# State-space scan: the exponentials of the decays read from the banks of the spread decays, in place of a second spreading product

## The chip, the cores and the metric

The kernel runs on one core of a Trainium2 chip. Its time is the device time of one execution in microseconds (us); lower is better. The engines of a core run side by side, each with its own queue in order: TensorE (PE; its weight loads are shown as PEld), VectorE (DVE), ScalarE (ACT), GpSimd (POOL) and SyncE (SP), which issues most DMA transfers. Matrix products are written into PSUM banks (here 128 partitions x 512 floats), from which DVE and ACT read.

## The reference, cut to what matters

One inference step of a decoder layer: an input projection, a Mamba-2 state-space scan beside an mLSTM, cross attention and a gated feed-forward block, for a prompt of 512 tokens and 8 samples of 8 tokens. The change lies in the prompt's state-space scan. Per chunk, with `cum` the running sum of the log decays:

```
cum = cumsum(lac)                         # per head, over the tokens t of a chunk
lmat = exp(cum[t] - cum[s])  for s <= t   # decay from token s to token t
y_intra = (C_t . B_s * lmat * dt_s) x_s
y_inter = (C_t . h) * exp(cum[t])         # h: the state at the chunk's start
y = y_intra + y_inter
```

There are 16 heads of 64 channels, so two heads fill the 128 partitions.

## The kernel before, in words

The kernel uses chunks of 128 tokens, four for the prompt. The head pairs are worked in two groups of four (`ssd_prompt(0)` and `ssd_prompt(1)`, L654). A group first transposes its inputs (`ps_bt`, `ps_xt`), forms the scores (`ps_cb`) and carries the states through the chunks (`ps_h`, L680; `hs`, L686/L687). Then comes the loop over its head pairs (L690):

- For each head k of the pair, a spreading product `ps_l` (L697, bf16, 80 rows) puts `cum` of this head, for all 512 tokens, on all 128 partitions of one bank. `cumst` holds `cum` split into three bf16 parts, `sel` picks the head.
- DVE makes `lm` from it in four pieces (L700), ACT takes the exponential (L702), DVE multiplies by the scores (L703).
- `ps_yi` (L710): y_intra, for both heads, each with 64 output columns of the array side by side.
- `ps_ec` (L715): a second spreading product, once more `cum`, for tokens 128 to 511, head 0 on partitions 0 to 63 and head 1 on partitions 64 to 127; ACT takes its exponential `ec` (L718).
- `ps_yn` (L721): C . h for chunks 1 to 3; DVE multiplies `ec` by it (L723), DVE adds `ps_yi` to the skip term (L724), POOL adds `ec` (L725).

`ec` has a single buffer, `lm` has two. All the banks named here come from one pool of three (`MP`, L139).

The order of the work is not written out by hand in this part: a scheduler arranges each engine's instructions from the program, with priorities in program order and its own estimates of durations. So TensorE's rows mix the scan with the products of the input projection (L215, L216 and L218: high part, low part of the activations, low part of the weights) and of the values (`ps_v`, L882), whose weights ACT casts (L191) and whose low parts DVE or POOL make (L198, L196). The samples' scan (`ps_hs` L813 with 32 output columns, `ps_hu` L824) and, behind the last head pair, the mLSTM (`ps_d` L960, `ps_n` L983/L985, `ps_c` L988; for the samples `ps_ss` L1024, `ps_nh` L1042/L1049 with 32 output columns, `ps_cu` L1056) are mixed in as well. In the mLSTM, ACT and DVE both read the bank `ps_d` (L962, L966).

Of the kernel before, what the change touches and what calls it, by code (L numbers as in the profile page):

```python
# [11 lines left out]
F32 = mybir.dt.float32  # L12
F32R = mybir.dt.float32r
BF16 = mybir.dt.bfloat16
AF = mybir.ActivationFunctionType
# [4 lines left out]
P = 128  # L20
T = 576
TP = 512
# [93 lines left out]
def build(nc, tc, ctx, I, O):  # L116
    V, A, G, S, TE = nc.vector, nc.scalar, nc.gpsimd, nc.sync, nc.tensor
    mm = TE.matmul
# [20 lines left out]
    def MP(name="m"):  # L139
        return pa.tile([P, 512], F32, name=name, tag="a")  # L140

    def BP(name="b"):
        return pb.tile([P, 512], F32, name=name, tag="b")
# [15 lines left out]
    def C16(k):  # L159
        a, b = _c16[k]  # L160
        return c16[:, a:b]

    def PAR(k, j=None, w=1):
        a, b = _cols[k]
        return par[:, a:b] if j is None else par[:, a + j:a + j + w]
# [42 lines left out]
    def gemm(ps, units, xh, xl, t0, n, k0=0, k1=None, order=None, late=0):  # L208


        tiles = [(hi[:, j * P:(j + 1) * P], lo[:, j * P:(j + 1) * P]) for hi, lo, nk in units for j in range(nk)]
        order = order or range(len(tiles))
        for i, k in list(enumerate(order))[k0:k1]:
            (wh, wl), ah, al = tiles[k], xh(k, t0, n), xl(k, t0, n)
            mm(ps, wh, ah, start=i == 0, stop=False)  # L215
            products.append(mm(ps, wh, al, start=False, stop=False))  # L216
            for c in range(late) if i == late - 1 else [i] if i >= late else ():
                m = mm(ps, tiles[order[c]][1], xh(order[c], t0, n), start=False, stop=c == len(tiles) - 1)  # L218
        return m
# [97 lines left out]
    sel = C16("sel")  # L317
# [74 lines left out]
    stop = gemm(ps0[2][1], [(*w2, KT)], U, UL, 256, 320, 0, NSS)  # L392
# [13 lines left out]
    stop = gemm(ps0[3][1], [(*w3, KT)], U, UL, 256, 320, 0, 2)  # L406
# [40 lines left out]
    cumst = bcp.tile([80, T], BF16, name="cumst")  # L447
# [166 lines left out]
    with tc.issue_after(products[140].ins), tc.high_priority(offset=1000):  # L614
# [9 lines left out]
        pse = MP("ps_en")  # L624
# [6 lines left out]
        pse = MP("ps_en2")  # L631
# [17 lines left out]
    sd = st.enter_context(tc.tile_pool(name="ssd", bufs=1, reuse_waits="tile"))  # L649
# [4 lines left out]
    def ssd_prompt(g):  # L654
        Bt, Ct = bc[:, g, :], bc[:, 2 + g, :]
        ps = MP("ps_bt")
        for c in range(4):
            TE.transpose(ps[:, c * P:(c + 1) * P], Bt[:, c * P:(c + 1) * P], ident)
        btok = sd.tile([P, 4, P], F32, name="btok", tag="btok")
        A.copy(btok, ps.rearrange("p (c k) -> p c k", c=4))  # L660
        ps = MP("ps_cb")
        for c in range(4):
            m = mm(ps[:, c * P:(c + 1) * P], Bt[:, c * P:(c + 1) * P], Ct[:, c * P:(c + 1) * P], start=True, stop=True,
                   skip_group_check=True)
        outer.append(m)
        cbs = sd.tile([P, 512], F32, name="cbs", tag="cbs")
        A.copy(cbs, ps)
        xdt, hs = [], [None]
        for c in range(4):
            ps = MP("ps_xt")  # L670
            for j in range(4):
                TE.transpose(ps[:, j * P:(j + 1) * P], xs[:, g * 4 + j, c * P:(c + 1) * P], ident)
            xd = sd.tile([P, 8, 64], F32, name="xdt", tag="xdt", bufs=4)
            V.tensor_tensor(xd, ps.rearrange("p (h k) -> p h k", h=8),
                            CT[:, c, 32 + 8 * g:40 + 8 * g].unsqueeze(2).to_broadcast([P, 8, 64]), op=ALU.mult)
            xdt.append(xd)
            xe = sd.tile([P, 8, 64], F32, name="xe", tag="xe", bufs=1)
            G.tensor_tensor(xe, xd, wend[:, c, 8 * g:8 * g + 8].unsqueeze(2).to_broadcast([P, 8, 64]), op=ALU.mult)
            ps = MP("ps_h")
            states.append(mm(ps, btok[:, c, :], xe.rearrange("p h k -> p (h k)"), start=True, stop=True))  # L680
            h = sd.tile([P, 8, 64], F32, name="hs", tag="hs", bufs=4)
            p3 = ps.rearrange("p (h k) -> p h k", h=8)
            if c == 0:
                V.tensor_copy(h, p3)
            else:
                G.tensor_tensor(h, hs[c], decp[:, c, 8 * g:8 * g + 8].unsqueeze(2).to_broadcast([P, 8, 64]), op=ALU.mult)  # L686
                V.tensor_tensor(h, h, p3, op=ALU.add)  # L687
            hs.append(h)
        S.dma_start(O["ssmp"][:, g * 512:(g + 1) * 512], hs[4].rearrange("p h k -> p (h k)"))
        for j in range(4):  # L690
            jj = g * 4 + j
            psi = MP("ps_yi")
            lms = []
            for k in range(2):
                h = 2 * jj + k
                psb = MP("ps_l")
                mm(psb, sel[:80, h:h + 1].to_broadcast([80, P]), cumst[:, 0:TP], start=True, stop=True)  # L697
                lm = sd.tile([P, 512], F32, name="lm", tag="tmp", bufs=2)
                for c in range(4):
                    V.scalar_tensor_tensor(lm[:, c * P:(c + 1) * P], psb[:, c * P:(c + 1) * P], ncum[:, c, h:h + 1],  # L700
                                           C16("maskp"), op0=ALU.add, op1=ALU.add)
                exps.append(A.activation(lm, lm, AF.Exp))  # L702
                mults.append(V.tensor_tensor(lm, lm, cbs, op=ALU.mult))  # L703
                lms.append(lm)
                if len(mults) == 8:
                    G.tensor_copy(sd.tile([P, 1], F32, name="lm0"), lm[:, 0:1])

            for c in range(4):
                for k in (1, 0):
                    m = mm(psi[64 * k:64 * k + 64, c * P:(c + 1) * P], xdt[c][:, 2 * j + k, :], lms[k][:, c * P:(c + 1) * P],  # L710
                       start=True, stop=True, skip_group_check=True)
            inner.append(m)
            pse = MP("ps_ec")
            for k in range(2):
                mm(pse[64 * k:64 * k + 64, 0:384], sel[:80, 2 * jj + k:2 * jj + k + 1].to_broadcast([80, 64]),  # L715
                   cumst[:, P:TP], start=True, stop=True, skip_group_check=True)
            ec = sd.tile([P, 384], F32, name="ec", tag="ec", bufs=1)
            A.activation(ec, pse[:, 0:384], AF.Exp)  # L718
            psn = MP("ps_yn")
            for c in range(1, 4):  # L720
                mm(psn[:, (c - 1) * P:c * P], hs[c][:, 2 * j:2 * j + 2, :].rearrange("p h k -> p (h k)"),  # L721
                   Ct[:, c * P:(c + 1) * P], start=True, stop=True, skip_group_check=True)
            V.tensor_tensor(ec, ec, psn[:, 0:384], op=ALU.mult)  # L723
            V.scalar_tensor_tensor(y[:, jj, 0:TP], xs[:, jj, 0:TP], PAR("dskip", jj), psi, op0=ALU.mult, op1=ALU.add)  # L724
            G.tensor_tensor(y[:, jj, P:TP], y[:, jj, P:TP], ec, op=ALU.add)  # L725

    inner, outer, exps, mults = [], [], [], []
    ssd_prompt(0)
    ssd_prompt(1)


# [15 lines left out]
    sd = st2.enter_context(tc.tile_pool(name="ssds", bufs=1, side="right", reuse_waits="tile"))  # L747
# [28 lines left out]
    for g in range(2):  # L776
        psb = BP("ps_ls")
        pb3 = psb.rearrange("p (h t) -> p h t", h=8)
        for h in range(8):
            mm(psb[:, h * TS:(h + 1) * TS], sel[:80, 8 * g + h:8 * g + h + 1].to_broadcast([80, P]), cumst[:, TP:T],  # L780
               start=h == 0, stop=h == 7, skip_group_check=True)
# [8 lines left out]
        for h in range(8):  # L790
            k, j = h % 2, (8 * g + h) // 2
            mm(psi[64 * k:64 * k + 64, j * TS:(j + 1) * TS], xdts[:, 8 * g + h, :], lm[:, h, :], start=True, stop=True,
               skip_group_check=True)
# [12 lines left out]
    for b in range(4):  # L806
# [3 lines left out]
        for g in range(2):  # L810
            for hb in (1, 0):
# [3 lines left out]
                   start=b == 0, stop=b == 3, skip_group_check=True)  # L815
# [141 lines left out]
    for h in range(4):  # L957
        q, k = qk[:, h, :], qk[:, 4 + h, :]
        psb = MP("ps_d")
# [10 lines left out]
        for c in range(4):  # L970
            mm(pss[:, c * P:(c + 1) * P], k[:, c * P:(c + 1) * P], q[:, c * P:(c + 1) * P], start=True, stop=True,
               skip_group_check=True)
# [37 lines left out]
    psb = BP("ps_ds")  # L1010
    pb3 = psb[:, 0:256].rearrange("p (h t) -> p h t", h=4)
    for h in range(4):
        mm(psb[:, h * TS:(h + 1) * TS], sel[:68, h:h + 1].to_broadcast([68, P]), sxst[:, TP:T], start=h == 0, stop=h == 3,
           skip_group_check=True)
# [22 lines left out]
    for hb in range(2):  # L1037
# [6 lines left out]
        for b in range(4):  # L1044
# [3 lines left out]
            for h in range(4):  # L1048
                mm(psn[32 * h:32 * h + 32, 0:257], qpad[:, h, bb, :], c0[:, h, 0:257], start=False, stop=b == 3,  # L1049
                   skip_group_check=True)  # L1050
# [1426 lines left out]
```

## Time and profile before

| | |
|---|---|
| median of 3 runs | 1074.99 us (1074.83 to 1075.98) |
| the profiled execution | 1074.69 us, of which 1072.9 us are its span |
| TensorE's granted clock, mean | 0.999 |
| the eight head pairs (first `ps_l` to the last add) | about 129 to 251 us of the span |

Rows of the chain give start (us), duration (us), engine, tile and line, and "xN" for N TensorE instructions; a float32 product counts as two of them. Rows of the timeline give start, duration, engine, line, operation, out<-in and, in brackets, how long the engine had been idle before and which instruction's end released it. Rows of a tile give the shortest, median and longest duration in ns.

### The profile page before, as it was taken

What the parts mean: (1) busy time and instruction counts of PE and PEld (TensorE: products, weight loads), DVE (VectorE), ACT (ScalarE), POOL (GpSimd) and SP (SyncE); (2) the same over time, 40 slices, a digit from 0 to 9 for tenths busy, and PEclk for the clock granted to TensorE, in tenths of its full rate; (3) what the DMA queues carried; (4) which work ended last, traced back from release to release, by engine and by line L of the source; (5) the groups of instructions that cost most, each with busy time, mean ns of one, the idle gap of its engine ahead of it and who ended that gap; (6) DMA issues with size and microseconds to landing.
All of it is one profiled execution on the core that took longest, in us unless ns stands there. A gap on an engine that the chain in (4) does not pass through costs nothing.

```text
span 1072.9 us, 20686 instructions
## 1 busy us (share of the span) xinstructions
PE 1063.1 (99%) x8096; PEld 1011.0 (94%) x8096; DVE 757.7 (71%) x1523; ACT 608.9 (57%) x1102; POOL 231.0 (22%) x305
## 2 busy tenths in 40 slices
PE   9999999999999999999999999999999999999997
PEld 8999887778999999999999989999999999999997
DVE  6798775658878774758755556766467887787556
ACT  7778523345654555655555445645566566656654
POOL 0454543313213111000154201100011111111000
PEclk9999999999999999999999999999999999999999
DMA  6776544425655349642468775743476687578532
GB/s 209 176 162 132 158 134 172 147 89 168 196 150 152 106 143 330 235 170 98 158 213 288 265 256 176 254 124 98 133 179 137 160 188 178 114 191 188 144 119 89
DMA packets 58965, 181.74 MB, mean 169 GB/s; under 512 B 6604, under 2 KB 12108, under 8 KB 58356
## 3 DMA queue, kind: packets, MB, share of 16 engines
q1 hardware_dynamic: 42884, 138.22, 38.7%
q0 software_dynamic: 15408, 41.43, 19.7%
q8 instruction: 63, 1.03, 0.4%
q10 hardware_dynamic: 576, 0.79, 0.2%
q14 instruction: 34, 0.28, 0.1%
HBM read 159.75 MB, written 20.65 MB: 168 GB/s over the span
## 4 chain that ended last, share of the span: by engine, by line
PE 98%; DVE 0%; DMA 0%; POOL 0%; issue 0%; ACT 0%; SPq 0%; DVEq 0%
PE ps_in L215 7%; PE ps_in L218 7%; PE ps_in L216 7%; PE ps_v L882 5%; PE ps_g L1946 3%; PE ps_u L1946 3%; PE ps_g L1945 3%; PE ps_o L218 3%; PE ps_o L216 3%; PE ps_u L1947 3%; PE ps_g L1947 3%; PE ps_o L215 3%; PE ps_u L1945 3%; PE ps_dn L1945 2%; PE ps_dn L1947 2%; PE ps_dn L1946 2%
## 5 line engine op out<-in xcount | busy, mean ns | idle before, releaser
L215 PE MATMUL ps_in<-uh,whi 128*128 128x320 f32 (+1 forms) x544 | 162.6, 299 | 0.0
L218 PE MATMUL ps_in<-uh,wlo 128*128 128x320 f32 (+1 forms) x544 | 161.6, 298 | 0.0
L216 PE MATMUL ps_in<-ul,whi 128*128 128x320 f32 (+1 forms) x544 | 161.1, 296 | 0.0
L191 ACT CAST whi<-raw 128x1024 fp32r<-128x1024 f32 (+1 forms) x104 | 105.4, 1015 | 93.3 <-PE ps_in L216 21.5
L198 DVE TENSOR_TENSOR wlo<-raw,whi 128x1024 fp32r<-128x1024 f32 (+2 forms) x97 | 95.3, 983 | 63.7 <-ACT whi L191 63.0
L215 PEld LDWEIGHTS ps_in<-uh,whi 128*128 128x128 f32 x544 | 102.3, 188 | 1.9 <-issue 0.8
L218 PEld LDWEIGHTS ps_in<-uh,wlo 128*128 128x128 f32 x544 | 102.2, 188 | 1.9 <-issue 1.3
L216 PEld LDWEIGHTS ps_in<-ul,whi 128*128 128x128 f32 x544 | 102.4, 188 | 0.5
L196 POOL DMA_DIRECT2D wlo<-win x31 | 27.2, 877 | 80.2 <-ACT wlo L195 69.9
L1945 PE MATMUL ps_g<-b,whi 128*128 128x288 f32 x144 | 42.4, 295 | 0.0
L1946 PE MATMUL ps_g<-b,whi 128*128 128x288 f32 x144 | 42.3, 294 | 0.0
L1946 PE MATMUL ps_u<-b,whi 128*128 128x288 f32 x144 | 42.2, 294 | 0.0
L1945 PE MATMUL ps_u<-b,whi 128*128 128x288 f32 x144 | 42.2, 294 | 0.0
L1905 DVE TENSOR_TENSOR wlo<-sw,whi 128x1024 fp32r<-128x1024 f32 (+1 forms) x26 | 29.6, 1139 | 16.8 <-ACT whi L1904 16.8
L1918 ACT CAST whi<-rawx 128x1024 fp32r<-128x1024 f32 (+1 forms) x26 | 25.6, 986 | 26.2 <-PE ps_dn L1946 13.3
L1895 ACT CAST whi<-raw 128x1024 fp32r<-128x1024 f32 (+1 forms) x26 | 25.6, 985 | 22.8 <-PE ps_g L1946 11.8
L215 PE MATMUL ps_xo<-qh,whi 128*128 128x288 f32 x128 | 38.2, 301 | 0.0
L216 PE MATMUL ps_xo<-ql,whi 128*128 128x288 f32 x128 | 37.8, 297 | 0.0
L218 PE MATMUL ps_o<-mixm_h,wlo 128*128 128x256 f32 (+1 forms) x128 | 37.5, 293 | 0.0
L216 PE MATMUL ps_o<-mixm_l,whi 128*128 128x256 f32 (+1 forms) x128 | 37.5, 293 | 0.0
L218 PE MATMUL ps_xq<-u2h,wlo 128*128 128x320 f32 (+1 forms) x128 | 37.5, 294 | 0.0
L218 PE MATMUL ps_o<-mixs_h,wlo 128*128 128x320 f32 (+1 forms) x128 | 37.4, 293 | 0.0
(788 smaller groups left out, 3855.6 us busy)
## 6 DMA issues: line engine op xcount, KB each, us to landing
raw<-win SPq DMA_DIRECT2D x35, 512.0 KB, 4.4
raw<-wout SPq DMA_DIRECT2D x17, 512.0 KB, 4.2
raw<-wxq SPq DMA_DIRECT2D x13, 512.0 KB, 4.7
raw<-wgate SPq DMA_DIRECT2D x13, 512.0 KB, 3.3
raw<-wup SPq DMA_DIRECT2D x13, 512.0 KB, 4.7
wlo<-win POOLq DMA_DIRECT2D x24, 256.0 KB, 5.6
kva<-vc SPq DMA_DIRECT2D x11, 512.0 KB, 5.9
raw<-wv SPq DMA_DIRECT2D x10, 512.0 KB, 4.0
```

The source lines that it names most:

```text
L191: casts.append(A.copy(hi[:, :n], raw[:, :n]))
L196: accs.append(G.dma_start(lo[:, a:b], src[:, a:b], accum_op=ALU.add))
L198: e.tensor_tensor(lo[:, a:b], raw[:, a:b], hi[:, a:b].bitcast(F32), op=ALU.subtract)
L215: mm(ps, wh, ah, start=i == 0, stop=False)
L216: products.append(mm(ps, wh, al, start=False, stop=False))
L218: m = mm(ps, tiles[order[c]][1], xh(order[c], t0, n), start=False, stop=c == len(tiles) - 1)
L882: mm(ps, a, b, skip_group_check=True, **kw)
L1895: s.c1 = A.copy(s.h1[:, s.all], s.r1[:, s.all])
L1905: V.tensor_tensor(s.l2[:, s.all], sw[:, s.all], s.h2[:, s.all].bitcast(F32), op=ALU.subtract)
L1945: mm(ps, wh, b[0][k], start=start and k == 0, stop=False, skip_group_check=True)
L1946: mm(ps, wh, b[1][k], start=False, stop=False, skip_group_check=True)
L1947: m = mm(ps, wl, b[0][k], start=False, stop=k == nk - 1, skip_group_check=True)
```

## The change

ACT takes the exponential of each head's half right from the `ps_l` bank: partitions 0 to 63 for the first head, 64 to 127 for the second. The second spreading product and its bank go; one exponential of 128 partitions becomes two of 64. `ec` is now written before `ps_yi` and not after it.

```
             psi = MP("ps_yi")
+            ec = sd.tile([P, 384], F32, name="ec", tag="ec", bufs=1)
             lms = []
             for k in range(2):
                 h = 2 * jj + k
                 psb = MP("ps_l")
                 mm(psb, sel[:80, h:h + 1].to_broadcast([80, P]), cumst[:, 0:TP], start=True, stop=True)
+                A.activation(ec[64 * k:64 * k + 64, :], psb[64 * k:64 * k + 64, P:TP], AF.Exp)
                 lm = sd.tile([P, 512], F32, name="lm", tag="tmp", bufs=2)
...
             inner.append(m)
-            pse = MP("ps_ec")
-            for k in range(2):
-                mm(pse[64 * k:64 * k + 64, 0:384], sel[:80, 2 * jj + k:2 * jj + k + 1].to_broadcast([80, 64]),
-                   cumst[:, P:TP], start=True, stop=True, skip_group_check=True)
-            ec = sd.tile([P, 384], F32, name="ec", tag="ec", bufs=1)
-            A.activation(ec, pse[:, 0:384], AF.Exp)
             psn = MP("ps_yn")
```

Behind the change the lines have other numbers: L697 becomes L698, L700 to L712 go up by two, and from L719 on they go down by four; the new exponentials are L699.

The scheduler moves rows with it. On TensorE, around the first head pair, before:

```order
L710 MATMUL ps_yi<-lm,xdt 64x128 x8
L715 LDWEIGHTS c_84
L715 MATMUL ps_ec<-cumst,c_84 64x384
L715 LDWEIGHTS c_84
L715 MATMUL ps_ec<-cumst,c_84 64x384
L721 MATMUL ps_yn<-bc,hs 128x128 x3
L813 MATMUL ps_hs<-h_1911,cpad 32x512
```

and after:

```order
L712 MATMUL ps_yi<-lm,xdt 64x128 x8
L717 MATMUL ps_yn<-bc,hs 128x128 x3
L698 LDWEIGHTS c_84
L698 MATMUL ps_l<-cumst,c_84 128x512
L809 MATMUL ps_hs<-h_1895,cpad 32x512
```

The two `ps_ec` rows are gone, and the first `ps_l` of the next head pair has moved up to stand right behind `ps_yn`; the same holds for each pair that follows another in its group, six in all. The fifth pair, the first of the second group, keeps its two `ps_l` one behind the other.

On DVE, between the second and the third head pair, before:

```order
L724 SCALAR_TENSOR_TENSOR xs<-xs,par,ps_yi 128x512 [waits PE_49]
L723 TENSOR_TENSOR ec<-ec,ps_yn 128x384 [waits PE_49,Activation_49]
L825 TENSOR_TENSOR h_1911<-h_1911,ps_hu 128x512 [waits PE_49]
L534 SCALAR_TENSOR_TENSOR qk<-ps_in,rxb 128x256 [waits PE_49]
L700 SCALAR_TENSOR_TENSOR lm<-ps_l,ncum,c_84 128x128 [waits DVE_49,PE_49]
```

and after:

```order
L720 SCALAR_TENSOR_TENSOR xs<-xs,par,ps_yi 128x512 [waits PE_49]
L719 TENSOR_TENSOR ec<-ec,ps_yn 128x384 [waits PE_49]
L821 TENSOR_TENSOR h_1895<-h_1895,ps_hu 128x512 [waits PE_49]
L534 SCALAR_TENSOR_TENSOR qk<-ps_in,rxb 128x256 [waits PE_49]
L702 SCALAR_TENSOR_TENSOR lm<-ps_l,ncum,c_84 128x128 [waits Activation_49]
```

The rows keep their places; the first piece of `lm` waits for ACT now, and the multiply of `ec` no longer does.

On TensorE, in the second block of the samples' mLSTM (`ps_nh`, four heads of 32 columns each), before:

```order
L1042 MATMUL ps_nh<-vts,ds__3162 32x257 x4
L1049 MATMUL ps_nh<-c_3330,qpad 32x257 x4
L1049 MATMUL ps_nh<-c_3351,qpad 32x257 x4
L1049 MATMUL ps_nh<-c_3372,qpad 32x257 x4
L1049 MATMUL ps_nh<-c_3393,qpad 32x257 x4
L1056 MATMUL ps_cu<-stb,km 128x258
```

and after:

```order
L1038 MATMUL ps_nh<-vts,ds__3146 32x257 x4
L1045 MATMUL ps_nh<-c_3314,qpad 32x257 x4
L1045 MATMUL ps_nh<-c_3335,qpad 32x257 x4
L1045 MATMUL ps_nh<-c_3356,qpad 32x257 x4
L1045 MATMUL ps_nh<-c_3377,qpad 32x257 x3
L1052 MATMUL ps_cu<-stb,km 128x258
L1045 MATMUL ps_nh<-c_3377,qpad 32x257
```

The last group of four is cut in two by a full-width product. In the first block a group is cut in the same way, there by three products of `ps_n` and `ps_c`. In the last third of the scan, `ps_ss` (64 output columns) now stands directly ahead of a `ps_yi`, where before other products lay between.

More of the change, by code (lines that the diff above doesn't have):

```diff
@@ L692, in ssd_prompt @@
             psi = MP("ps_yi")
+            ec = sd.tile([P, 384], F32, name="ec", tag="ec", bufs=1)
             lms = []
@@ L697, in ssd_prompt @@
                 mm(psb, sel[:80, h:h + 1].to_broadcast([80, P]), cumst[:, 0:TP], start=True, stop=True)
+                A.activation(ec[64 * k:64 * k + 64, :], psb[64 * k:64 * k + 64, P:TP], AF.Exp)
                 lm = sd.tile([P, 512], F32, name="lm", tag="tmp", bufs=2)
@@ L712, in ssd_prompt @@
             inner.append(m)
[L713 to L718, printed above, removed]
             psn = MP("ps_yn")
```

## Prediction, made before the changed kernel was run

> **What bounds the kernel now.** I read the page of the profile first: the shares of the engines, then the chain that ended last.
>
> ```profile
> PE 1063.1 (99%) x8096; PEld 1011.0 (94%) x8096; DVE 757.7 (71%) x1523; ACT 608.9 (57%) x1102; POOL 231.0 (22%) x305
> ...
> PE 98%; DVE 0%; DMA 0%; POOL 0%; issue 0%; ACT 0%; SPq 0%; DVEq 0%
> ```
>
> TensorE is busy nearly all of the span, and the chain of work that ended last runs on it for 98%. So the time is the sum of what TensorE has to do, plus any gap in it; work of the other engines counts only where TensorE comes to wait for it. Next I asked for the two stretches in which the eight head pairs of the scan lie.
>
> ```profile
> 130.00:185.00 55.00, 55.00 (x398) 44.88 (x397) 37.48 (x75) 17.41 (x29) 20.33 (x14) 1.00 0.45 148
> 185.00:255.00 70.00, 70.00 (x428) 55.81 (x426) 45.66 (x90) 32.33 (x49) 21.63 (x26) 1.00 0.41 132
> ```
>
> After the times of the stretch stand the busy times of PE, weight load, DVE, ACT and POOL, then the granted clock. PE has no gap at all in 125 us at full clock; ACT is busy 49.7 of 125 us. A TensorE instruction taken away here shortens the span by its own share, and a wait of TensorE lengthens it by the whole wait.
>
> **The removed product.** The chain in order of time gives each piece's own share of the span. This is the first head pair and what follows it, and then the last pair.
>
> ```profile
> 138.03 1.02 PE ps_yi L710 x16
> 139.05 0.17 PE ps_ec L715 x2
> 139.22 0.86 PE ps_yn L721 x6
> 140.08 0.99 PE ps_hs L813 x8
> 141.08 0.35 PE ps_in L218
> ...
> 141.95 0.14 PE ps_in L218
> ...
> 248.40 0.17 PE ps_ec L715 x2
> ```
>
> The two halves of `ps_ec` together take 0.17 us. There are eight head pairs, so the change takes 8 x 0.17 = 1.36 us off TensorE. Could more go with it? Behind `ps_hs` the next L218 takes 0.35, an ordinary one 0.14: about 0.20 is a price for what went before. `ps_hs` holds no bf16 product, only narrow outputs (32 columns of the array), so I read the 0.20 as the price of going from narrow to full width. `ps_yn` will hold such a price in its 0.86, and since `ps_yi` (64 columns) still goes to `ps_yn` (128), it stays. The removal is worth 1.36, with 8 x (0.17 + 0.20) = 2.96 as its other end. The Trainium skill, page "TensorEngine Tiling (Array Packing)", Key Properties, says that changing the tiling mode drains the engine. By it too the price stays and the sum is the same; the opposite reading, that the price goes with the bf16 product, is a rival below.
>
> **ACT's side.** Eight exponentials of 128x384 become sixteen of 64x384.
>
> ```profile
> L718 ACT ACTIVATE ec<-ps_ec x8: 491/491/492, 139.3 to 248.7; 128x384 f32<-128x384 f32 x8
> ```
>
> Three copies out of banks, by the timeline:
>
> ```profile
> 177.97 0.59 ACT L660 COPY btok<-ps_bt 128x512 f32<-128x512 f32 x1 [1.28 <-PE ps_bt L658]
> ...
> 203.27 0.58 ACT L906 COPY vts<-ps_v 64x512 f32<-64x512 f32 x1
> ...
> 234.86 0.69 ACT L910 ACTIVATE vt<-ps_v,rx_r 128x512 f32<-128x512 f32 x1 [0.30 <-PE ps_v L882]
> ```
>
> A copy of 64 partitions takes as long as one of 128 (0.58 and 0.59), so each half costs 0.49: ACT gains 8 x 0.49 = 3.9 us of work in 125, of which it idles 75. That alone costs nothing; if that idle time were gone, it would be 3.9 us.
>
> **The new wait.** The bank of `ps_l` now has two readers, ACT and DVE. The kernel already has such a bank, `ps_d` in the mLSTM part:
>
> ```profile
> 285.47 0.51 ACT L962 ACTIVATE qs<-ps_d 128x384 f32<-128x384 f32 x1
> 286.02 1.12 DVE L966 SCALAR_TENSOR_TENSOR dm<-ps_d,CT,c 128x128 f32<-128x128 f32 x4 [0.20 <-ACT qs L962]
> ```
>
> They take turns: DVE starts 0.04 after ACT's end. The order shows the same turn: each first DVE row of a `ps_l` bank now waits for Activation in place of PE. The Trainium skill, page "PSUM — Partial Sum Buffer", section on bank collisions, says that two engines may not touch the same bank and quadrant at once, two reads included, and that semaphores must keep them apart. The row agrees; by this rule sharing a bank is not free, which speaks against the change.
>
> So 0.49 + 0.04 = 0.53 us enter the chain second `ps_l` -> spread -> exponential -> multiply -> `ps_yi`. Here is that chain in the last head pair, and the multiplies of all pairs.
>
> ```profile
> 243.18 0.39 PE L697 MATMUL ps_l<-cumst,c 80*128 80x512 bf16 x1
> 243.61 2.16 DVE L700 SCALAR_TENSOR_TENSOR lm<-ps_l,ncum,c 128x128 f32<-128x128 f32 x8 [2.38 <-PE ps_l L697]
> ...
> 243.85 0.39 PE L697 MATMUL ps_l<-cumst,c 80*128 80x512 bf16 x1
> 244.77 0.63 ACT L702 ACTIVATE lm<-lm 128x512 f32<-128x512 f32 x1 [4.40 <-DVE lm L700]
> 245.69 1.47 DVE L703 TENSOR_TENSOR lm<-lm,cbs 128x512 f32<-128x512 f32 x2
> 245.80 0.63 ACT L702 ACTIVATE lm<-lm 128x512 f32<-128x512 f32 x1 [0.40 <-DVE lm L700]
> ...
> 247.31 1.09 PE L710 MATMUL ps_yi<-lm,xdt 128*64 128x128 f32 x16
> ```
> ```profile
> L703 DVE TENSOR_TENSOR lm<-lm,cbs x16: 674/683/2074, 132.8 to 246.5; 128x512 f32<-128x512 f32 x16
> ```
>
> From the start of `ps_l` to its first reader 0.43; ACT's half 0.49; then 0.04; four DVE pieces 1.12; 0.03 to ACT; 0.63; 0.05 to DVE; one multiply 0.68; 0.15 to PE (247.31 less the end of the multiplies, 245.69 + 1.47). Sum 3.62 us from the second `ps_l` to `ps_yi`. TensorE fills this time with ordinary products, and the order has moved `ps_l` among them. The first `ps_l` of a pair now comes right behind the previous `ps_yn`; the second stays, or comes later. Where the filling is shorter than 3.62, TensorE waits at `ps_yi`. The rows for three pairs:
>
> ```profile
> 156.81 0.39 PE L697 MATMUL ps_l<-cumst,c 80*128 80x512 bf16 x1
> ...
> 159.04 0.68 DVE L825 TENSOR_TENSOR h<-h,ps_hu 128x512 f32<-128x512 f32 x1
> ...
> 159.63 1.29 DVE L703 TENSOR_TENSOR lm<-lm,cbs 128x512 f32<-128x512 f32 x2
> ...
> 160.97 0.77 PE L710 MATMUL ps_yi<-lm,xdt 128*64 128x128 f32 x10
> ```
> ```profile
> 229.76 4.15 PE ps_v L882 x18
> 233.91 0.45 PE ps_l L697 x2
> ...
> 238.52 1.02 PE ps_yi L710 x16
> ```
>
> Last pair: 247.31 - 243.85 = 3.46, and by the order two 320-wide products of 0.14 fewer stand in it: 3.18, so 0.44 late. Seventh pair: from the second `ps_l` (233.91 + 0.45 / 2 = 234.14) to 238.52 it is 4.38, less five products of 4.15 / 18 = 0.23: 3.23, so 0.39 late. Third pair: 160.97 - 156.81 = 4.16, less three products of 0.14: 3.74; but on DVE the state update (L825) still stands between the spread and the two multiplies, which end 159.63 + 1.29 - 159.04 = 1.88 after its start. The chain is then 0.43 + 0.49 + 0.04 + 1.12 + 1.88 + 0.15 = 4.11: 0.37 late. Behind the waiting DVE row stand the low parts of weights (L198) and copies out of banks, for which TensorE's products wait; they go late by the same half us, and a unit of weights lasts TensorE 24 products for one half of the tokens, at least 24 x 0.14 = 3.4 us, so I cost that at nothing. In the other pairs the same count leaves 4.3 us or more, for a chain of 3.62. Together 1.20 us of new TensorE waits. Bounds: none (DVE and ACT gain by the earlier first half, and fill is longer than I count) to 3 x 0.69 more, if ACT's copy of a value bank (L910) gets in front of each second half.
>
> A second new wait: ACT's first half of a pair rewrites the single `ec` buffer, so it waits for POOL's add of the pair before.
>
> ```profile
> 154.61 0.54 DVE L723 TENSOR_TENSOR ec<-ec,ps_yn 128x384 f32<-128x384 f32 x1
> ...
> 155.22 1.02 POOL L725 TENSOR_TENSOR xs<-xs,ec 128x384 f32<-128x384 f32 x1 [5.35 <-DVE ec L723]
> ```
>
> `ec` is free at 156.24. Behind ACT's half on its queue stand weight casts (L191) and the second half; but the first DVE spread of this pair began only at 156.97 before, and ACT's half would end at 156.24 + 0.49 = 156.73. I cost it at nothing; if the spread were wanted at once, DVE would stand from 155.15 to 156.73, 1.6 us.
>
> **What the scheduler moves besides.** In the first third of TensorE's rows the order shifts; behind that it is the same. Two shifts change how often TensorE changes width. The narrow `ps_nh` products ran four side by side:
>
> ```profile
> 261.90 0.57 PE ps_nh L1042 x8
> 262.46 0.57 PE ps_nh L1049 x8
> 263.04 0.63 PE ps_n L985 x2
> ...
> 264.10 0.43 PE ps_n L983 x2
> ...
> 264.65 1.44 PE ps_nh L1049 x24
> 266.09 0.34 PE ps_in L218
> ```
>
> Three groups of four take 1.44, so a group is 0.43 and leaving the narrow width 0.14, plus 0.20 on the next piece (0.63 against 0.43, 0.34 against 0.14). Now one group in each half of the samples is cut into three and one. A lone one should take as long as four: 0.43 more each, and the second block gets one more change of width, 0.34: together 1.20. Bounds: 0, if the lone one runs beside its neighbours, to 2 x 0.57 + 0.34 = 1.48. The other way, `ps_ss` (narrow) now stands directly ahead of a `ps_yi`, which saves a change, 0.20 (0 to 0.34). The other moves are swaps among full-width pieces, in which no such price shows; I cost them at nothing.
>
> **Sum.** -1.36 + 1.20 (`ps_yi` waits) + 1.20 (`ps_nh`) - 0.20 = +0.84 us. The profiled execution took 1074.69 us (span 1072.9, and 1.79 around it); 1074.69 + 0.84 = 1075.5. The median of three runs is 0.30 above the profiled one, well inside what I can resolve; about 0.2% (2.15 us) is what a measurement here can tell from no change: under 1072.8 is faster, over 1077.1 slower.
>
> **Rivals.**
> 1. *The chain grows at all three pairs (slower).* ACT's in-order queue holds the second half behind L910, which waits for TensorE's own value product, as the [0.30 <-PE ps_v] of its row shows. Each wait grows by 0.69: +0.84 + 2.07 = 2.9, 1077.6. It decides from where ACT reaches the second half 0.69 late in each of them; against it, L910 stands there in only one of the three. Chance 0.20.
> 2. *Only the removed product counts.* `ps_yi` is not late and lone `ps_nh` ride along: -1.36 - 0.20 = -1.56, 1073.1. For it: chains ran close to TensorE before too, and left no gap. Against: the 0.53 that they now gain. Chance 0.17.
> 3. *The price of width goes with the bf16 product*, and nothing else comes: -2.96 - 0.20 = -3.2, 1071.5. Against it is the 0.35 behind `ps_hs`. Chance 0.07.
> 4. *The change does not do what it says*: excluded by the order, in which all sixteen `ps_ec` rows are gone.
>
> My forecast has 0.56; its own range is 1074.3 (no lone `ps_nh` price) to 1077.1. The likeliest time is 1075.5; the range 1073.0 to 1077.8 takes in rivals 1 and 2 and the bounds of the waits, without rival 3. Faster has rival 3's 0.07; slower has rival 1's 0.20 and 0.02 of the forecast's upper end; same has the rest, 0.71.
>
> **What would show it.** The chain after should show `ps_yn` directly behind `ps_yi` with 0.86 again; PE waits for DVE (lm) ahead of `ps_yi` in the third, seventh and eighth pair, 0.4 each; `DVE lm <- ACT ec` among the waits; a lone `ps_nh` x2 of about 0.4. I am wrong if `ps_yn` falls to 0.66, if TensorE has no wait ahead of `ps_yi`, or if a wait of over 1 us stands elsewhere.

## The result and the profile after

| | before | after |
|---|---|---|
| median of 7 runs | 1074.99 us | 1079.12 us (1077.82 to 1079.88) |
| profiled execution (span) | 1074.69 us (1072.9) | 1078.66 us (1076.8) |

The ratio is 1.0037, with a 95% interval of 1.0024 to 1.0049: the kernel is slower by some 4 us. One of the seven executions of before took 2218.64 us and is left out of the ratio. The forecast was 1075.5, range 1073.0 to 1077.8; the time lies above it.

The page of after, first the engines, then the chain that ended last:

```profile
PE 1063.4 (99%) x8080; PEld 1010.8 (94%) x8080; DVE 759.2 (71%) x1523; ACT 611.4 (57%) x1110; POOL 235.0 (22%) x305
...
PE 93%; DVE 3%; DMA 2%; ACT 1%; issue 1%; POOL 0%; SPq 0%; DVEq 0%; ACTq 0%
```

The sixteen matmuls are gone (8096 to 8080), but TensorE's share of the chain fell from 98% to 93%: DVE, DMA and ACT now stand in it. The two stretches of the scan:

```profile
130.00:185.00 55.00, 54.41 (x393) 44.25 (x392) 38.24 (x75) 18.71 (x32) 20.75 (x15) 1.00 0.48 158
185.00:255.00 70.00, 68.50 (x409) 55.27 (x409) 45.36 (x88) 33.93 (x53) 20.21 (x21) 1.00 0.38 118
```

Before, TensorE had no gap there; now it has 0.59 and 1.50 us. The waits of TensorE name them (us in total, times, longest):

```profile
PE ps_yi L712 <- DVE lm L705: 2.0, 4, 1.0
...
PE ps_g L1941 <- ACT f_ffn L2111: 0.6, 1, 0.6
PE ps_o L215 <- DVE tmp L1129: 0.3, 1, 0.3
PE ps_u L1941 <- ACT whi L1891: 0.2, 1, 0.2
```

The first row is the forecast's new wait. The others belong to the output projection and to the feed-forward part, hundreds of us behind the change, where the forecast saw nothing.

**Where the time went.** I took each TensorE instruction of the profiled execution and subtracted the start of the same instruction in that of before. For example the transposes at the end (before, then after):

```profile
L2309 PE MATMUL ps_ft<-c,f_ffn x14: 271/273/273, 1061.8 to 1064.7; 128*128 128x128 f32 x14
```
```profile
L2305 PE MATMUL ps_ft<-c,f_ffn x14: 271/272/273, 1065.7 to 1068.6; 128*128 128x128 f32 x14
```

They start 3.9 us later. What each stretch of the program adds to this lateness, in us, for this run and for all kernels that follow:

| kernel | start to 128 | 128 to 400: scan, mLSTM | 400 to 775 | 775 to 800 | sum | ratio to before (95%) |
|---|---|---|---|---|---|---|
| after | +0.36 | +2.06 | +0.20 | +1.34 | +3.96 | 1.0037 (1.0024 to 1.0049) |
| after, a second time (a0) | -0.22 | +1.80 | +0.04 | +2.07 | +3.69 | 1.0031 (1.0018 to 1.0043) |
| two `ec` (e1) | -0.07 | +1.48 | -0.03 | +1.79 | +3.17 | 1.0023 (1.0013 to 1.0032) |
| no product (e2) | +0.02 | -0.28 | +0.34 | +1.08 | +1.16 | 1.0005 (0.9996 to 1.0014) |
| second reader alone (e3) | +0.23 | +9.05 | +1.65 | 0.00 | +10.93 | 1.0075 (1.0061 to 1.0089) |
| DVE first (e4) | -0.52 | +0.58 | +0.62 | +2.09 | +2.77 | 1.0011 (1.0002 to 1.0020) |
| code back (e5) | -0.12 | +2.94 | +0.04 | 0.00 | +2.86 | 1.0029 (1.0018 to 1.0040) |
| code ahead (e6) | +2.25 | -0.01 | +0.26 | +1.26 | +3.76 | 1.0019 (1.0010 to 1.0028) |
| whole groups (e7) | +0.53 | +0.70 | +0.80 | +1.42 | +3.45 | 1.0019 (1.0010 to 1.0029) |
| three mends (e8) | +0.30 | -0.60 | +0.14 | +0.02 | -0.14 | 1.0005 (0.9992 to 1.0018) |
| values behind (e9) | -0.47 | +1.53 | +0.06 | +1.45 | +2.57 | 1.0026 (1.0013 to 1.0038) |

The stretches are those of one execution, and the first one differs by about 1 us among kernels whose start is the same: that part is chance. The second and the fourth stretch are what had to be explained. The forecast had +0.84 in the second and nothing in the fourth. The second can be cut once more, at 254 us of before: the scan to there adds +0.82 in after, +0.52 in a0 and -1.52 in e2; the mLSTM behind it adds +1.24, +1.28 and +1.24, but +0.01 in e7 and nothing in e3.

### The profile page after: what moved, and what is told of

Its sections match the earlier page's. It is cut to its first block, busy times and chain, and to the rows that moved or that the text cites. A ratio compares the mean times of both kernels' runs of the same rounds, so it can differ in the third digit from the quotient of the medians.

```text
span 1076.8 us, 20656 instructions
## 1 busy us (share of the span) xinstructions
PE 1063.4 (99%) x8080; PEld 1010.8 (94%) x8080; DVE 759.2 (71%) x1523; ACT 611.4 (57%) x1110; POOL 235.0 (22%) x305
## 4 chain that ended last, share of the span: by engine, by line
PE 93%; DVE 3%; DMA 2%; ACT 1%; issue 1%; POOL 0%; SPq 0%; DVEq 0%; ACTq 0%
PE ps_in L215 6%; PE ps_in L218 6%; PE ps_in L216 6%; PE ps_u L1942 3%; PE ps_u L1941 3%; PE ps_v L878 3%; PE ps_u L1943 3%; PE ps_o L218 3%; PE ps_o L215 3%; PE ps_o L216 3%; PE ps_g L1942 3%; PE ps_g L1941 3%; PE ps_g L1943 3%; PE ps_dn L1941 2%; PE ps_dn L1943 2%; PE ps_dn L1942 2%
## 5 line engine op out<-in xcount | busy, mean ns | idle before, releaser
L215 PE MATMUL ps_o<-mixs_h,whi 128*128 128x320 f32 (+1 forms) x128 | 37.5, 293 | 0.3 <-DVE tmp L1129 0.3
```

## The experiments

**The change unchanged, a second time (a0).** 

> The kernel after unchanged, a second time: which of its losses come back. If they belong to the program (order and places of code loads), then against the kernel before the late ps_yi are in pairs 3, 4, 7 and 8 again with about 0.23, 0.47, 1.05 and 0.46 us, the mLSTM part loses again what it lost, and the step at 780 us is there again (1.0 to 2.1 us); the 0.36 us at the start need not come back. Ratio 1.0024 to 1.0049 again. If they are chance of one run, some are missing here.

The late `ps_yi`, the loss up to 400 us and the step at 780 us came back; the 0.36 at the start did not. Gaps of TensorE ahead of `ps_yi`, beyond those of before, in pairs 3, 4, 7 and 8: 0.23, 0.47, 1.05 and 0.46 us in after (2.21), 0.23, 0.48, 0.77 and 0.50 here (1.98). These are the gaps from the last matmul's start to `ps_yi`'s, less the same gap in before.

**The removal without a second reader (e2).** ACT's exponential reads another tile:

```
-            pse = MP("ps_ec")
-            for k in range(2):
-                mm(pse[64 * k:64 * k + 64, 0:384], ...)
-            A.activation(ec, pse[:, 0:384], AF.Exp)
+            A.activation(ec, cbs[:, 0:384], AF.Exp)
```

> The kernel before without the product ps_ec; ACT's one exponential of 128x384 stays but reads the scores in SBUF (cbs) in its place, so y_inter is scaled wrongly: the removal alone, without a second reader of ps_l. By its order it has the same two cut groups of ps_nh behind the scan as the kernel after. Theory A: the scan gains the eight products, -1.36 us, ps_yi is as little late as before; behind 255 us the moved order costs what it cost in the kernel after (1.0 to 2.0 us up to the end of the mLSTM); together -0.4 to +0.7 us on the kernel before. Rival B (the waits at ps_yi come from the moved order of TensorE's rows, not from the second reader): ps_yi is late here too, +3 us or more. Rival C (what was lost behind the scan was chance of one run, and ps_nh x2 costs nothing): -1.4 us.

Theory A held up to the end of the mLSTM: no wait of `ps_yi` is left among TensorE's waits, the scan gains 1.52, the mLSTM loses 1.24 of it, and up to 400 us the kernel is 0.28 faster than before. After and its repeat lie 2.34 and 2.08 above it, which is the price of the second reader and agrees with the gaps of 2.21 and 1.98. Rival C fell; it wanted -1.4. But the step behind 775 us is here too:

```profile
PE ps_g L1941 <- ACT f_ffn L2111: 0.3, 1, 0.3
```

So the step needs no late scan, and no second reader.

**The second reader without the removal (e3).** Before, with an added exponential per head from the `ps_l` bank into a tile `ex`:

```
                 mm(psb, sel[:80, h:h + 1]..., cumst[:, 0:TP], ...)
+                A.activation(ex[64 * k:64 * k + 64, :], psb[64 * k:64 * k + 64, P:TP], AF.Exp)
```

> The kernel before with everything kept, the product ps_ec too, and beside it ACT's two halves of 64x384 read from each ps_l bank into a tile that nobody reads (bf16, and ec is bf16 too, for room): the second reader alone, without removal; behind the scan its order has whole groups of ps_nh like the kernel before. Theory A: the halves make DVE and so ps_yi late as in the kernel after, +2.2 us (1.2 to 3.2), nothing more is lost behind the scan. Rival B (moved order, not the reader): 0 to +0.5 us. If the loss behind the scan follows from lateness in the scan and not from the order there, it comes here too: +3.5 us or more.

Up to 400 us all of it is in the scan, none behind 255 us, and none comes at 780, as theory A says; but it is 9.05 us and not 2.2. With the `ps_ec` bank still there, both `ps_l` of a pair stay nearly together in the order, so both halves and both spreads lie in one chain, and DVE's state updates go late behind it. TensorE then waits for those too (waits; then two windows of PE busy time, with the granted clock third from the end):

```profile
PE ps_hu L826 <- DVE h L827: 2.8, 2, 2.2
PE ps_yi L712 <- DVE lm L705: 2.8, 3, 1.6
```
```profile
162.00:166.00 4.00, 1.82 (x10) 1.17 (x11) 3.63 (x6) 1.08 (x3) 0.00 (x0) 0.68 0.67 217
166.00:170.00 4.00, 4.00 (x23) 3.30 (x20) 1.30 (x2) 0.49 (x1) 0.26 (x1) 0.50 0.79 301
```

In the wait of 2.2 us (162.2 to 164.4 us of the span) the granted clock fell to 0.50, where it stayed from 163.4 to 170.2, and the products in it took twice their time. By an estimate that costs at most half of the 5.9 us from 164.4 on, 2.9 of the 9.05; theory A did not have it. The rest, some 6 us, is still far over 2.2.

**DVE reads the bank first (e4).** The same two readers, the other turn:

```
-                A.activation(ec[64 * k:64 * k + 64, :], psb[64 * k:64 * k + 64, P:TP], AF.Exp)
                 lm = sd.tile(...)
 ...
                 exps.append(A.activation(lm, lm, AF.Exp))
+                A.activation(ec[64 * k:64 * k + 64, :], psb[64 * k:64 * k + 64, P:TP], AF.Exp)
```

> The kernel after, but ACT's half is issued behind the exponential of lm, so that DVE reads the ps_l bank first and ACT's half stands in no chain to ps_yi; bank and sum stay those of the kernel after. Theory A: the late ps_yi go (under 0.5 us over the kernel before in all pairs), -1.36 us of products gone, the cut groups of ps_nh and what follows them stay: like the run without product, -0.4 to +0.7 us on the kernel before. Rival B: about as slow as the kernel after, +3 us or more. Rival D (the bank is held longer by the late reader, so the next ps_l waits for it): waits of TensorE ahead of ps_l in place of those ahead of ps_yi.

No `ps_yi` waits for DVE any more, and no `ps_l` for a bank (rival D falls). Up to 400 us it is 0.58 us slower than before, 0.86 more than e2, about the 0.8 of one new wait at `ps_hu` (its `bm` stands in ACT's queue behind a cast that waited 2.16 for weights); the step at 780 us is there again:

```profile
PE ps_g L1941 <- ACT f_ffn L2111: 1.3, 1, 1.3
...
PE ps_hu L820 <- ACT bm L815: 0.8, 1, 0.8
```

What cost 2 us was not that ACT reads the bank, but that it reads it ahead of DVE. The Trainium skill, page "PSUM — Partial Sum Buffer", section on bank collisions, says that two engines may not read the same bank and quadrant at once. e4 and after take turns alike, and the order of the turns is worth 2.21 us in pairs 3, 4, 7 and 8 against 0.03, by the same gaps. The kernel gains less by it, 1.2 to 1.5 us up to 400 us, since the wait at `ps_hu` takes 0.8 back.

**Two buffers of `ec` (e1).** `bufs=1` becomes `bufs=2`, and F32 becomes BF16. 

> The kernel after with two buffers of ec; to find room for them they hold bf16, so y_inter is rounded to bf16 here. ACT's first half of a pair then no longer waits for POOL's add of the pair before (22.6 us of such waits in the kernel after). Theory A (the chain over the second ps_l): in the kernel after no late ps_yi comes from this wait, since DVE reached the first spread of pairs 4 and 7 later anyway; so the time stays that of the kernel after, about +4 us on the kernel before, and the TensorE waits at ps_yi keep some 2 us over it. Rival P (POOL's add is what makes ACT late, and ACT the rest): the waits at ps_yi fall by over half, the time is +2.5 us or less.

Between the two theories. The gap of pair 3 went back to that of before, pair 7's excess fell from 1.05 to 0.47, pair 4's rose from 0.47 to 0.71; the stretch to 400 us gains 0.3 to 0.6. So POOL's add, which the forecast costed at nothing, seems to be a small part of the waits; what the change of `ec` to bf16 does by itself was not measured.

**One ACT instruction moved (e9).** Why is pair 7 later than forecast? The chain in after that ends in its `ps_yi`:

```profile
230.00 3.39 DMA raw<-win
...
233.46 1.06 ACT whi L191
...
234.55 0.63 ACT wlo L195
235.18 0.52 ACT lm L704
235.70 0.58 ACT vt L906
...
236.30 0.50 ACT ec L699
...
236.82 1.14 DVE lm L702 x4
...
239.49 1.09 PE ps_yi L712 x16
```

It does not begin at the second `ps_l`, as the forecast's chain did, but at a transfer of weights: in ACT's queue the second half stands behind a cast that waits for weights, a low part, an exponential and a value copy. The excess of pair 7 follows the landing of this transfer: counted from the lateness at 128 us, it lands 0.31 us earlier in the repeat and 0.87 later in e5, and the excess is 0.28 smaller and 0.86 larger. I moved that last copy:

```
+                with tc.issue_after(halves[13].ins) if g and c == 3 else ExitStack():
                     A.activation(vt4[:, c, 2 * g:2 * g + 2, 0:256], p2, AF.Copy, ...)
```

> The kernel after with one instruction of ACT moved: the last value copy of the prompt (vt, L906) is issued behind the second half of the seventh pair, not ahead of it. Theory Q (in pair 7 it is ACT's queue that makes the half late: a cast that waits for weights, a low part, an exponential, then this copy of 0.67): DVE waited 0.40 for the half there, so ps_yi of pair 7 comes 0.40 earlier, 0.65 late in place of 1.05, and the whole 0.4 us sooner than the kernel after. Rival (the chain starts at the second ps_l, as forecast): no change of pair 7's wait, since ps_l landed long before.

On DVE, the repeat of after first (its row waits for the half), then this kernel (its row waits for nothing):

```profile
235.94 1.13 DVE L702 SCALAR_TENSOR_TENSOR lm<-ps_l,ncum,c 128x128 f32<-128x128 f32 x4 [0.40 <-ACT ec L699]
```
```profile
235.46 1.12 DVE L702 SCALAR_TENSOR_TENSOR lm<-ps_l,ncum,c 128x128 f32<-128x128 f32 x4
```

DVE's 0.40 is gone, and pair 7's gap is 0.72. In the repeat it was 0.98 and in after 1.26, so it falls by 0.26 or 0.54; the transfer lands as in after (0.05 earlier), which makes 0.54 the nearer one, with 0.40 expected. The whole time shows nothing that can be told from after. Theory Q's mechanism is shown, its size only roughly. Pair 4, which the forecast had left out, has a chain of the same kind, on DVE in after:

```profile
166.60 1.12 DVE L702 SCALAR_TENSOR_TENSOR lm<-ps_l,ncum,c 128x128 f32<-128x128 f32 x4
168.68 1.23 DVE L198 TENSOR_TENSOR wlo<-raw,whi 128x1024 fp32r<-128x1024 f32 x1 [0.97 <-ACT whi L191]
169.83 0.68 DVE L705 TENSOR_TENSOR lm<-lm,cbs 128x512 f32<-128x512 f32 x1
170.43 1.12 DVE L702 SCALAR_TENSOR_TENSOR lm<-ps_l,ncum,c 128x128 f32<-128x128 f32 x4
```

Before, both spreads ran as one block of 2.16 ahead of the low part of the weights; now the second spread, queued behind the multiply of the first head, comes behind it, and the low part itself waits 0.97 for a cast. From the second `ps_l` to `ps_yi` pair 4 takes 5.23 us, not 3.62. But in e4 a low part stands between the spreads too, and waits 1.43, and there `ps_yi` of pair 4 waits for nothing. So the low part alone is not the cause; no experiment took that one apart.

**Whole groups of `ps_nh` (e7).** The second group of the first half is issued behind the second `ps_n`, and the `ps_cu` of a half are written behind all its `ps_nh`:

```
+            with tc.issue_after(ns_[1].ins) if bb == 1 else ExitStack():
                 for h in range(4):
                     mm(psn[32 * h:32 * h + 32, 0:257], qpad[:, h, bb, :], c0[:, h, 0:257], ...)
+        for b in range(4):
+            cus(b)
```

> The kernel after with its ps_nh products in whole groups of four again: the second group of the first half is issued behind the second ps_n, and the ps_cu of a half are written behind all its ps_nh. The scan keeps its order. Two lone products of 0.43 go and one change of width of 0.34, one other change of width comes in the first block (four products of L21x between): theory A expects -0.9 us on the kernel after, about +3.2 us on the kernel before, and ps_nh at 5.0 us in all in place of 5.96. Rival (a lone ps_nh is not what the mLSTM part lost): the part from 255 to 390 us keeps its loss, about +4 us on the kernel before.

The first block in after, then in e7 (chain; a float32 product counts as two, so a group of four is x8, and x14 and x18 are where one is cut):

```profile
259.71 0.57 PE ps_nh L1038 x8
260.27 1.00 PE ps_nh L1045 x14
261.27 0.63 PE ps_n L979 x2
261.90 0.43 PE ps_c L984 x2
262.33 0.43 PE ps_n L979 x2
262.77 1.42 PE ps_nh L1045 x18
264.19 0.34 PE ps_in L215
```
```profile
259.76 0.57 PE ps_nh L1039 x8
260.33 0.57 PE ps_nh L1061 x8
260.90 0.34 PE ps_in L215
...
262.98 1.44 PE ps_nh L1061 x24
```

Cut, the `ps_nh` of the block take 0.57 + 1.00 + 1.42 = 2.99; whole, 0.57 + 0.57 + 1.44 = 2.58. A lone product costs the 0.4 of a group, as forecast; in both blocks `ps_nh` takes 5.97 in after and 5.01 in e7. From 128 to 400 us the kernel gains 1.1 to 1.36 on the two executions of after, a little more than the 0.9 expected, and behind the scan nothing of the loss is left (+0.01). The `ps_cu` were moved too, so of the gain only the 0.96 at `ps_nh` is surely the groups' own.

**The step at 780 us (e5 and e6).** Nothing in that part differs in order. But one transfer of weights does. DMA from the issue of `raw<-wgate` to ACT's first use of it, before and then after (packets and MB of each queue; KB and us from issue to landing):

```profile
q1 hardware_dynamic: 144, 0.52, 45.7%
...
raw<-wgate SPq DMA_DIRECT2D x1, 512.0 KB, 3.1
```
```profile
q1 hardware_dynamic: 144, 0.52, 27.1%
q8 instruction: 1, 0.02, 1.1%
...
raw<-wgate SPq DMA_DIRECT2D x1, 512.0 KB, 5.3
```

In after, a packet of the `instruction` queue falls into the transfer, which lands 2.2 us later: 135 of its 144 packets have started by 770.4 us, and the last nine come one after another up to 772.4. The buffer is free late, so the next transfer is issued late, its cast is late, and behind it in ACT's queue so is the copy `f_ffn` for which `ps_g` waits (chain of after):

```profile
775.59 5.26 DMA raw<-wup
...
780.93 0.07 ACT wacc L1886
...
781.89 0.41 ACT f_ffn L2111
```

Before, `raw<-wup` was issued at 770.78. The page of after counts these packets:

```profile
q8 instruction: 63, 1.03, 0.4%
```

That is 16 KB every 17 us, and 2 x 8080 matmuls and weight loads over 63 are 256 for each. My reading: they are TensorE's program, and since the change takes instructions out of it (16 products and 16 weight loads by the page's counts, and two more by the trace's), each later piece is loaded at another place of the work. The trace agrees: the median number of matmuls and weight loads that start between two such packets is 252 to 257 in all twelve kernels. Two kernels test it, in opposite directions:

```
     for _ in range(NWARM):
         mm(psw[:, 0:256], wz[:, 0:128], wz, ...)
+    for _ in range(17):                                    # e5, added to after
+        mm(psw[:, 0:1], wz[:, 0:128], wz[:, 0:1], ...)
```
```
-NWARM = 19
+NWARM = 2                                                  # e6, in before
```

> The kernel after with 17 one-column warm-up products added behind the 19 at the start, where TensorE waits for its first inputs anyway: TensorE's program then has as many instructions as that of the kernel before (34 more: a weight load and a product each), so that every 16 KB piece of its code is loaded at the place in the program where the kernel before loads it. The order of all that follows is that of the kernel after. Theory L (the step of 1.34 us at 780 us, ps_g waiting for ACT and this for the weights, comes from a code load that falls into a transfer of weights): the step is gone, the other losses stay, about +2.7 us on the kernel before. Rival (the step follows from the moved order or the lateness): it stays, about +4 us.

> The kernel before with 2 warm-up products in place of 19: TensorE's program is 34 instructions shorter, as in the kernel after, and nothing else moves. Theory L (code loads): against the kernel before, TensorE loses 1.1 to 2.1 us between 775 and 790 us, ps_g waits for ACT there, and nothing between 130 and 700 us. Rival (moved order): no step there. The start may itself change by -0.5 to +2 us, since the warm-up is shorter; the step is read from the profile, not from the whole time.

e5 has the order of after and no step; the transfer lands in 3.1 again:

```profile
raw<-wgate SPq DMA_DIRECT2D x1, 512.0 KB, 3.1
```

e6 has the order of before and the step, with a code packet in the transfer and after's wait at `ps_g`:

```profile
q8 instruction: 1, 0.02, 1.1%
...
raw<-wgate SPq DMA_DIRECT2D x1, 512.0 KB, 5.1
```
```profile
PE ps_g L1945 <- ACT f_ffn L2115: 0.3, 1, 0.3
```

Over all kernels it holds: in before, e3, e5 and e8 no such packet falls between the issue and the landing, and there is no step; in the other eight one does, and the step is 1.08 to 2.09 us. Between 130 and 400 us e6 differs from before by 0.01. Its 2.25 us lie at the start, where the shorter warm-up is: TensorE is busy from 8 to 12 us of the span in both, but starts 20 products there against 34 in before. By the medians e5 is 2.5 us slower than before, as the +2.7 expected; but its scan lost 0.9 more than after's, nearly all of it ahead of pair 7, whose gap grew to 2.12, so the agreement is in part luck:

```profile
PE ps_yi L714 <- DVE lm L707: 2.9, 4, 1.8
```

There a code load came at 229.4 us, just as `raw<-win`, the transfer that feeds pair 7 (see e9), was issued at 229.5; it took 4.3 us to land, 3.4 in after. That the load made it late was not tested by itself. The Trainium skill, page "DMA: Bandwidth & Descriptors", section "Issuing engines are not separate DMA queues", says that transfers of all issuing engines run on the same 16 DMA engines and interleave; the 3.1 and 5.3 us agree, and show it for code as well.

**Three mends at once (e8).** e4's turn, e7's groups and e5's 17 products. 

> Three mends at once: ACT's half behind the exponential of lm (DVE reads the bank first), whole groups of ps_nh, and 17 one-column warm-up products that put the code loads back. If the three causes add up: products gone and width paid by ps_yi -0.9, no late ps_yi, mLSTM part +0.3, no step at 780 us: -0.5 us on the kernel before (-1.5 to +0.5). If they don't (the bank held longer by the late reader, another code load that now falls badly): +1 us or more.

The causes add up: -0.60 to 400 us, 0.02 at 780 us. The time is that of before, 1.0005 (0.9992 to 1.0018), and the chain is TensorE's again:

```profile
PE 98%; DVE 1%; DMA 0%; ACT 0%; POOL 0%; issue 0%; SPq 0%; DVEq 0%
```

That is the best version found, and it beats after but not before: 1.36 us of removed product are about 0.13% of the time and were partly spent again (0.8 at `ps_hu`).

## Why the prediction was wrong, by its own steps

- **The removed product, -1.36: right.** In e2, which has no second reader either, the scan gains 1.52. In the chain of after `ps_yn` stands directly behind `ps_yi` with 0.86 again, so the price of width stayed and rival 3 fell:

```profile
138.39 1.02 PE ps_yi L712 x16
139.42 0.86 PE ps_yn L717 x6
```

- **The `ps_nh` groups, +1.20: right; `ps_ss`, -0.20: not tested.** Two lone groups cost about 0.4 each; the mLSTM loses 1.24 to 1.28 in after, its repeat and e2, and 0.01 in e7. In e2 no `ps_ss` stands ahead of a `ps_yi`, so there the forecast's terms give -1.36 + 1.20 = -0.16, and e2 measured -0.28.
- **The new TensorE waits, +1.20: too small, about 2.1 to 2.3.** The mechanism was right (TensorE waits for `lm` ahead of `ps_yi`; e4 shows that ACT's turn ahead of DVE is the cause). The step that failed is "In the other pairs the same count leaves 4.3 us or more, for a chain of 3.62", with the chain itself: it was taken to begin at the second `ps_l`. In pair 8, where it does, the forecast of 0.44 met 0.46. In pair 3 it was 0.37 against 0.23. In pair 7 the queue of ACT stood ahead of the half with a cast that waited for weights: 1.05 against 0.39, and 0.77 in the repeat. That is rival 1's copy (L910, now L906) in the one pair where the forecast saw it, and ahead of the copy a cast that waits for a transfer. In pair 4 the filling was there as counted, but the chain took 5.23 us: 0.47 late against nothing. What makes up the difference there stays open (see e9).
- **ACT's wait for POOL's add, nothing: not quite.** Worth 0.3 to 0.6 in e1, which made `ec` bf16 as well.
- **"behind that it is the same": this step hid the second error.** The order behind is the same, but TensorE's program is shorter, and so its code is loaded at other places. One load falls into a transfer that has no slack: +1.34 and +2.07. The forecast's bounds held no term for it, and without it the time would not have left the range: 0.84 with a wait term of 2.2 would be 1.84, and 1074.69 + 1.84 = 1076.5 lies inside. The longer waits had their part: by the profiled execution, 1078.66, either miss alone would have left it inside, at 1077.3 without the step of 1.34 and at 1077.7 without the 1.0 us of longer waits.
- **What would show it:** the waits at `ps_yi` are there, in pair 4 too, and so are `DVE lm <- ACT ec` (7.0 us in seven waits) and the lone `ps_nh` of about 0.4. "A wait of over 1 us stands elsewhere" came true in the repeat and in e4 at `ps_g` (1.3), and stood for the cause that was missing.

Open: the up to 1.65 us between 400 and 775 us, where waits for transfers come and go (in e4 `ps_os` waits 0.6 for `kva`), were not taken apart. How much of e3's 9.05 is the halved clock was estimated, not measured by itself.

## What to carry to other kernels

When a bank gets a second reader, let the one whose result is on the chain read first: the same work made TensorE wait 2 us in one turn and nearly nothing in the other, though 0.8 came back at another place. A wait is sized from what stands ahead in the reader's own in-order queue, transfers included, not only from the producer. And where an engine is 99% busy with weights arriving just in time, removing instructions can shift its code loads against the weights for the rest of the run, as it did here; look at the transfer that got slower before looking for a cause in the change.

## What the runs showed of the hardware

Unexpected were two things. With a code load of 16 KB inside it, one transfer of 512 KB (`raw<-wgate` near 767 us) landed after 4.8 to 5.6 us, in eight kernels; in the four without, after 3.1 to 3.3. Not every load costs as much: `raw<-win` near 230 us took 3.1 to 3.6 us with one in its last 0.6 us, and 3.2 to 3.4 with none. And in one wait of TensorE of 2.2 us (with 0.65 shortly ahead of it) its granted clock was halved for 6.8 us in e3, while in waits up to 1.8 us, as in e5, it was not. The Trainium skill, page "TensorE: Matmul & The Clock Gate", section "Why this matters for your kernels", gives a bound of about 3 us for such gaps; here the clock fell after less.
